# Attention scores in two fp32r passes with the query's two parts stacked in the rows, and the gate projection on four column tiles of the array

## The chip, the cores and the metric

The kernel runs on one NeuronCore of a Trainium2 chip. The metric is device time in microseconds (us) of one execution, lower is better; a kernel's time is the median over its runs. TensorE is called PE here (PEld is its weight load), VectorE DVE, ScalarE ACT, GpSimd POOL, and SP is the queue that issues most DMAs.

## The reference, cut to what matters

The program computes two transformer blocks of two layers each on 256 tokens of width 1024, in fp32. The change touches only the first layer of the first block. That layer projects the normed input `h` to 5,000-odd columns, sends one part through an mLSTM branch and the other through a sparse attention branch (NSA), and projects both back:

```python
proj = h @ w_in + b_in
ya = mlstm_branch(m_cols, ...)      # 4 + 4 gate columns: i_pre, f_pre
yb = nsa_branch(n_cols, ...)        # 24 gate columns: 8 heads x 3
...
s_s = jnp.einsum('bgrqd,bgqnd->bgrqn', q_blk, ks_g)   # selected keys
p_s = masked_softmax(s_s, tok_ok[:, :, None])
...
s_w = jnp.einsum('bgrqd,bgnd->bgrqn', q_blk, kwb)     # window keys
p_w = masked_softmax(s_w, wmask)
```

There are 8 query heads of 64 numbers in 2 groups; each group has its own keys. With 256 tokens both branches see all earlier tokens, so each is a plain causal attention over up to 256 keys. The 32 gate columns (4 input gates, 4 forget gates, 24 branch gates) are ordinary columns of `w_in`.

## The kernel before

**Layout.** Activations lie transposed: 128 partitions of features, 256 tokens in the free dimension, eight such slices for the width of 1024 (`xT`). A weight matrix is read in pieces of 128 x 1024; two pieces make one 1 MB DMA into a tile `raw` (three buffers, `load_raw`, L152). ACT rounds a piece to fp32r, `whi` (L161), DVE forms the rest, `wlo` (L162), and PE makes three one-pass products per 128 rows of the width: high by high, low by high, high by low (L221 to L223, or L206 to L208 where tokens are the output's rows). So one column tile of 128 columns costs one ACT cast, one DVE subtraction and 24 matmuls of 256 columns. Plain fp32 operands also can be multiplied; the trace shows such a matmul as two records.

**The layer.** `even_layer` (L391) runs over `EV_TILES` (L27), the order of its column tiles. `columns` (L458) projects them, `evict` (L411) scales the result by the token's norm (`norm.scaled`, tile `nt`, L310) and adds the bias. Tile `G` holds the 32 gate columns, spread to the rows 0 to 3, 32 to 35 and 64 to 87 of a 128-column tile whose other columns are zero; it goes to `gsb`. The mLSTM branch (`mlstm`, L521) and the attention (`nsa`, L597) are generators; `even_layer` runs their pieces between groups of column tiles.

**The attention.** `nsa` first normalises keys and queries in `nqk` (rows 0 to 63 are group 0, rows 64 to 127 group 1; slices 0 to 3 are the heads' queries, 4 the selected keys, 5 the window keys). `kblk` (L665) holds, for each group, its keys in its own 64 rows and zeros in the others, so that a matmul over all 128 rows with both groups' queries gives one group's scores. Then for two query blocks `qb` of 128 tokens, for four head pairs `j`, for two groups `g`: a score matmul (L748, 256 columns for the first block and 512 for the second), a mask (L749), the row maximum on DVE (L750, L751), two exponentials on ACT (L753), the scaling (L761, L763), transposes on PE (L769), a copy on ACT (`nPT`, L771) and the products with the values (tile `long`, L776, L777). Score and transpose share the two PSUM banks of `mbank(0)`.

**What sets the order.** Each engine works off its instructions in order. That order is not written by hand: the program is emitted in the order of the code with priorities, and a scheduler places each instruction by its own estimate of times. So a change in one place moves instructions on all engines behind it. `ada` (L338) is a long list of 96 DVE reductions over 512 KB weights (`araw`, L350, L351) that belong to the second block; `step` hands them out one by one from the first layer on, at raised priority, and `finish` forces them before they are needed.

**The layer behind.** `hgrn_layer` (L786) runs nine levels of small matmuls twice (L858, `hq`, `hk`, `hAC`), each between column tiles.

## Time and profile before

| | |
|---|---|
| median of 3 runs | 827.72 us (826.15 to 830.46) |
| profiled execution, its own time | 830.03 us |
| span in the profile | 828.2 us |
| mean granted clock of PE | 0.992 |
| PE busy | 807.2 us, 97% of the span |
| DVE busy | 672.1 us, 81% |
| ACT busy | 520.3 us, 63% |

"Busy" of PE is the time in which at least one matmul record is open, and records overlap, so it says when PE was fed and not that it ran at its peak. The granted clock is given as a share of 2.4 GHz. The chain of waits follows the execution back from its last instruction: each piece is what the piece after it waited for.

### The profile page before, as it was taken

The numbers are of one execution on the slowest core, as the hardware profiler recorded it, in microseconds if no ns is written. First come the engines' busy times: TensorE is split into PE (matmuls) and PEld (weight loads), VectorE is DVE, ScalarE is ACT, GpSimd is POOL, SyncE is SP. The second block draws the span as 40 slices with busy tenths as digits, with TensorE's granted clock in tenths as the row PEclk, the third lists the DMA queues.
The fourth block names the chain that finished last, engine by engine and source line by source line (L and its number), as shares of the span: only waits on it lengthen the run. The fifth ranks groups of instructions, "written<-read, shape, count | busy, mean of one in ns | idle before, by whom it ended". The sixth has DMA issues, their size and how long they took to land.

```text
span 828.2 us, 16357 instructions
## 1 busy us (share of the span) xinstructions
PE 807.2 (97%) x6534; PEld 740.2 (89%) x6534; DVE 672.1 (81%) x1257; ACT 520.3 (63%) x934; POOL 4.9 (1%) x19
## 2 busy tenths in 40 slices
PE   8999999989999999999999999999999999999995
PEld 8968977879999987999999888889999999988884
DVE  7689988899899989999999888876679777755552
ACT  7556765676876556658776734446657777754441
POOL 0000000001000000000000000000000000000000
PEclk9999999999999999999999999999999999999998
DMA  9644566657885777568878889874445454555521
GB/s 345 254 168 144 185 224 221 236 198 251 293 290 204 249 255 258 203 231 271 293 278 285 287 314 316 310 265 154 160 146 204 153 203 163 195 187 175 198 102 51
DMA packets 34635, 184.64 MB, mean 223 GB/s; under 512 B 3968, under 2 KB 4608, under 8 KB 19200
## 3 DMA queue, kind: packets, MB, share of 16 engines
q1 hardware_dynamic: 33696, 181.96, 62.8%
q10 hardware_dynamic: 864, 1.65, 0.6%
q8 instruction: 51, 0.84, 0.4%
q14 instruction: 24, 0.20, 0.1%
HBM read 182.55 MB, written 1.05 MB: 222 GB/s over the span
## 4 chain that ended last, share of the span: by engine, by line
PE 66%; DMA 13%; DVE 12%; ACT 5%; issue 4%; DVEq 0%; ACTq 0%; SPq 0%
PE g L221 12%; PE g L222 12%; DMA araw<-in_ada_w_dram 12%; PE g L223 12%; PE g L1035 9%; PE g L1036 5%; DVE wlo L162 4%; DVE araw L351 3%; ACT whi L161 2%; PE g L207 1%; PE g L208 1%; PE g L206 1%; PE m L858 1%; PE m L748 1%; PE long L776 1%
## 5 line engine op out<-in xcount | busy, mean ns | idle before, releaser
L221 PE MATMUL g<-ahi,whi 128*128 128x258 f32 (+1 forms) x1256 | 360.1, 289 | 4.0 <-ACT ahi L213 2.5
L222 PE MATMUL g<-alo,whi 128*128 128x258 f32 (+1 forms) x1256 | 357.6, 286 | 0.1
L223 PE MATMUL g<-ahi,wlo 128*128 128x258 f32 (+1 forms) x1256 | 356.6, 285 | 0.0
L162 DVE TENSOR_TENSOR wlo<-raw,whi 128x1024 fp32r<-128x1024 f32 (+1 forms) x238 | 288.6, 1216 | 73.5 <-ACT whi L161 72.9
L161 ACT CAST whi<-raw 128x1024 fp32r<-128x1024 f32 (+1 forms) x238 | 246.2, 1043 | 160.1 <-PE g L222 68.0
L221 PEld LDWEIGHTS g<-ahi,whi 128*128 128x128 f32 x1256 | 238.7, 191 | 8.7 <-ACT ahi L213 3.1
L222 PEld LDWEIGHTS g<-alo,whi 128*128 128x128 f32 x1256 | 240.2, 191 | 2.1 <-issue 0.8
L223 PEld LDWEIGHTS g<-ahi,wlo 128*128 128x128 f32 x1256 | 239.3, 191 | 1.7 <-issue 1.0
L1035 PE MATMUL g<-ghl,whi 128*128 128x512 f32 x512 | 179.9, 394 | 0.6 <-DVE nb L1020 0.6
L1036 PE MATMUL g<-ghl,wlo 128*128 128x256 f32 x512 | 143.5, 280 | 2.7 <-DVE wlo L162 2.4
L351 DVE CUSTOM_DVE_ANT_0 araw<-araw,row_c,prm 128x1024 f32<-128x1024 f32 x96 | 122.5, 1279 | 23.5 <-DMA araw<-in_ada_w_dram 23.3
L1035 PEld LDWEIGHTS g<-ghl,whi 128*128 128x128 f32 x512 | 96.0, 187 | 23.3 <-issue 0.7
L1036 PEld LDWEIGHTS g<-ghl,wlo 128*128 128x128 f32 x512 | 96.0, 187 | 4.0 <-DVE wlo L162 3.9
L310 DVE TENSOR_TENSOR nt<-g,nrstd 128x256 f32<-128x256 f32 x133 | 55.5, 419 | 17.3 <-PE g L223 16.9
L1021 ACT ACTIVATE nt<-nt,nb 128x256 f32<-128x256 f32 x64 | 32.4, 507 | 21.3 <-DVE nb L1020 21.3
L280 ACT ACTIVATE ahi<-xT,gains 128x256 fp32r<-128x256 f32 x32 | 16.2, 507 | 36.2 <-DVE xT L330 32.3
L214 DVE TENSOR_TENSOR ghl<-nt,ghl 128x256 fp32r<-128x256 f32 x64 | 27.0, 423 | 3.8 <-ACT ghl L213 1.4
L1022 ACT ACTIVATE nt<-nt 128x256 f32<-128x256 f32 x64 | 26.7, 418 | 1.9
L213 ACT CAST ghl<-nt 128x256 fp32r<-128x256 f32 x64 | 25.9, 406 | 1.9
L208 PE MATMUL g<-wlo,ahi 128*128 128x512 f32 (+1 forms) x64 | 24.3, 379 | 0.0
L206 PE MATMUL g<-whi,ahi 128*128 128x512 f32 (+1 forms) x64 | 24.2, 378 | 0.0
L286 ACT ACTIVATE sq<-xT 128x256 f32<-128x256 f32 x56 | 22.3, 405 | 3.0 <-DVE xT L330 3.0
(290 smaller groups left out, 758.7 us busy)
## 6 DMA issues: line engine op xcount, KB each, us to landing
raw<-in_mlp_w_dram SPq DMA_DIRECT2D x64, 1024.0 KB, 5.0
araw<-in_ada_w_dram SPq DMA_DIRECT2D x96, 512.0 KB, 5.1
raw<-in_ev_w_in_dram SPq DMA_DIRECT2D x17, 1024.0 KB, 6.1
raw<-in_od_w_in_dram SPq DMA_DIRECT2D x16, 1024.0 KB, 6.0
raw<-in_sgu_w_in_dram SPq DMA_DIRECT2D x8, 1024.0 KB, 4.7
raw<-in_ev_w_out_dram SPq DMA_DIRECT2D x4, 1024.0 KB, 4.9
raw<-in_od_w_out_dram SPq DMA_DIRECT2D x4, 1024.0 KB, 4.9
raw<-in_sgu_w_out_dram SPq DMA_DIRECT2D x4, 1024.0 KB, 4.7
```

The lines of the kernel that those rows point to most:

```text
L161: S.copy(hi[:, c], r[:, c])
L162: V.tensor_sub(lo[:, c], r[:, c], hi[:, c])
L206: PE.matmul(ps[tb], pair.hi(k)[:, ts_], wh[:, j, :], start=st, stop=False)
L208: PE.matmul(ps[tb], pair.hi(k)[:, ts_], wl[:, j, :], start=False, stop=sp)
L221: PE.matmul(ps, wh(k), ah(k), start=st, stop=False)
L222: PE.matmul(ps, wh(k), al(k), start=False, stop=False)
L223: PE.matmul(ps, wl(k), ah(k), start=False, stop=sp)
L310: V.tensor_tensor(t, ps[:, :T], self.r, op=ALU.mult)
L351: V.tensor_tensor_reduce(raw, raw, crow, 1.0, P("ada_b", layer * 48 + c), ALU.mult, ALU.add, mod[:, c : c + 1])
L1021: S.activation(r, r, AF.Relu, bias=b)
L1035: PE.matmul(ps, wh[:, k, :], a.rearrange("p s t -> p (s t)"), start=st, stop=sp, skip_group_check=True)
L1036: PE.matmul(ps[:, :T], wl[:, k, :], a[:, 0, :], start=False, stop=sp, skip_group_check=True)
```

## The change

Two things are changed, both in the first layer.

The scores: `q2` holds a query's rounded high part in the rows of its own group and the low part in the 64 rows of the other group, where `kblk` used to have zeros. `kblk` holds the keys' high part in both halves of the rows, and in a second slice their low part in both. Two fp32r matmuls, one per key part, give all four products. `q2` (in the memory of `cX`) is made for two head pairs at a time, by two ACT casts and two DVE subtractions of 64 x 256. `kblk` is made by six ACT copies and two DVE subtractions of 64 x 512 in place of a DVE memset and two DVE copies.

The gates: their 32 columns are loaded apart (`ev_w_g`, 128 KB, in the memory of `mE`), multiplied by the norm's gain on DVE, and projected with the unsplit `xT` by eight fp32 matmuls of 32 columns, four of them on the four column tiles of the array and four more added on top. A further fp32 matmul with a matrix of ones and zeros, `spread`, adds the four partial sums and puts each gate to its row. `G` leaves the column tiles, and with the padding tile that it needed, one 1 MB load and one split go.

```diff
-                if name == "G":
-                    V.tensor_scalar(gsb, t, gbias, None, op0=ALU.add)
...
+            def gates():
...
+                raw = mk(et, [128, 256], F32, "mE")
+                nc.sync.dma_start(raw, io["ev_w_g"])
+                wg = raw.rearrange("p (k n) -> p k n", n=32)
+                V.tensor_tensor(wg, wg, norm.gain[:, :, None].to_broadcast([128, KT, 32]), op=ALU.mult)
+                ps = gbank()[:, :T]
+                for k in range(KT):
+                    c = 32 * (k % 4)
+                    PE.matmul(ps[c : c + 32], wg[:, k, :], xT[:, k, :], start=k < 4, stop=k > 3, tile_position=(0, c))
+                t = norm.scaled(ps)
+                spread = mk(et, [128, 128], F32, "mqk")
+                G.memset(spread, 0.0)
+                for a, b, n in ((0, 0, 4), (32, 4, 4), (64, 8, 24)):
+                    S.copy(spread[:, a : a + n], lvl[:, 0, b : b + n])
+                pg = mbank(1)[:, :T]
+                PE.matmul(pg, spread, t, start=True, stop=True)
+                V.tensor_scalar(gsb, pg, gbias, None, op0=ALU.add)
...
-            columns(EV_TILES[6:11])
+            columns(EV_TILES[6:8])
+            gates()
+            columns(EV_TILES[8:10])
...
-        kblk = mk(ev, [128, 2, 2, T], F32, "kblk")
-        V.memset(kblk, 0.0)
+        kblk = mk(ev, [128, 2, 2, 2, T], F32R, "kblk")
         for g in range(2):
-            V.tensor_copy(kblk[64 * g : 64 * g + 64, g, :, :], nqk[64 * g : 64 * g + 64, 4:6, :])
+            own, other = slice(64 * g, 64 * g + 64), slice(64 - 64 * g, 128 - 64 * g)
+            k = nqk[own, 4:6, :]
+            for p in (own, other):
+                S.copy(kblk[p, g, 0], k)
+            V.tensor_sub(kblk[own, g, 1], k, kblk[own, g, 0])
+            S.copy(kblk[other, g, 1], kblk[own, g, 1])
...
+                if j % 2 == 0:
+                    q2 = mk(et, [128, 2, 2, 128], F32R, "cX", bufs=1)
+                    for g in range(2):
+                        own, other = slice(64 * g, 64 * g + 64), slice(64 - 64 * g, 128 - 64 * g)
+                        q = nqk[own, j : j + 2, qs]
+                        S.copy(q2[own, g], q)
+                        V.tensor_sub(q2[other, g], q, q2[own, g])
...
-                    PE.matmul(pv, nqk[:, j, qs], kblk[:, g, :, 0:n], start=True, stop=False)
+                    for part in range(2):
+                        PE.matmul(pv, q2[:, g, j % 2, :], kblk[:, g, part, :, 0:n], start=part == 0, stop=False)
```

How the order moves, at three places. On PE, where tile `G` ends and the tokens' tile `sv` begins (`g_464` is `G`'s bank, `g_498` that of `sv`; 21 more rows of `G` stand ahead of these), before:

```order
L221 MATMUL g_464<-ahi_129,whi_467 128x256
L222 MATMUL g_464<-alo_130,whi_467 128x256
L223 MATMUL g_464<-ahi_129,wlo_468 128x256
L206 MATMUL g_498<-whi_500,ahi_113 128x256
L207 MATMUL g_498<-whi_500,alo_114 128x256
L208 MATMUL g_498<-wlo_501,ahi_113 128x256
```

The same place now, from the last row of the tile ahead (`g_432`):

```order
L223 MATMUL g_432<-ahi_129,wlo_434 128x256
L481 MATMUL g_467<-xT_73,mE_464 32x256 x8
L206 MATMUL g_486<-whi_490,ahi_113 128x256
L207 MATMUL g_486<-whi_490,alo_114 128x256
L208 MATMUL g_486<-wlo_491,ahi_113 128x256
L206 MATMUL g_486<-whi_490,ahi_113 128x256
L207 MATMUL g_486<-whi_490,alo_114 128x256
L488 MATMUL m_85_483<-nt_476,mqk_478 128x256
L208 MATMUL g_486<-wlo_491,ahi_113 128x256
```

The 24 rows became eight and, five rows of `sv` later, the matmul with `spread`. On ACT, between the last copies of head pair 2 and the exponentials of head pair 3 of the first query block, before:

```order
L771 COPY nPT_1358<-m_242_1355 128x256
L771 COPY nPT_1368<-m_244_1365 128x256
L380 ACTIVATE mo_176<-nt_1742,hbias_181 128x256
L753 ACTIVATE A_1376,nsm_892<-m_248_1377,nnmx_891 128x128 x2
L580 ACTIVATE w_263_1445<-m_262_1443 128x256
```

Now:

```order
L806 COPY nPT_1367<-m_244_1364 128x256
L806 COPY nPT_1377<-m_246_1374 128x256
L777 CAST cX_1497<-nqk_177 64x256 x2
L788 ACTIVATE A_1385,nsm_885<-m_250_1386,nnmx_884 128x128 x2
L788 ACTIVATE A_1385,nsm_885<-m_251_1394,nnmx_884 128x128 x2
```

The two casts of `q2` for the second query block stand straight ahead of the exponentials. On DVE, at the maxima of head pair 2 of the second query block, before:

```order
L351 ISA araw_2316,mod_10_89<-araw_2316,row_c_396,prm_71 128x1024
L351 ISA mod_10_89 128x1
L750 TENSOR_REDUCE nmx_1459<-m_308_1624 128x2
L750 TENSOR_REDUCE nmx_1459<-m_309_1631 128x2
L751 TENSOR_SCALAR nnmx_1460<-nmx_1459 128x2
```

Now:

```order
L162 TENSOR_TENSOR wlo_1920<-raw_1881,whi_1919 128x1024
L785 TENSOR_REDUCE nmx_1470<-m_303_1594 128x2
L785 TENSOR_REDUCE nmx_1470<-m_304_1602 128x2
L786 TENSOR_SCALAR nnmx_1471<-nmx_1470 128x2
L778 TENSOR_TENSOR cX_1644<-nqk_177,cX_1644 64x256
L786 TENSOR_SCALAR nnmx_1471<-nmx_1470 128x2
L778 TENSOR_TENSOR cX_1644<-nqk_177,cX_1644 64x256
```

An `ada` reduction went from the place ahead of the maxima, and two subtractions of `q2` stand around the second bias. Over the whole DVE queue, 21 `ada` reductions stood ahead of the attention's first product with `nz` (L445) before and 17 stand there now; between that row and the last row of `hiv` (L846) in the next layer it is 27 and 28. On SP the load of the gate weights stands behind the third load of `ev_w_in`, and one load of `ev_w_in` fewer follows.

## Rows read from the trace of the kernel before

**Rows 1.** The page: busy of PE, and its granted clock in 40 slices.

```profile
PE 807.2 (97%) x6534; PEld 740.2 (89%) x6534; DVE 672.1 (81%) x1257; ACT 520.3 (63%) x934; POOL 4.9 (1%) x19
PEclk9999999999999999999999999999999999999998
```

**Rows 2.** Busy by stretch: length, then us busy and (records) of each engine, clock, DMA.

```profile
30.00:40.00 10.00, 10.00 (x86) 10.00 (x85) 5.51 (x9) 3.43 (x5) 0.00 (x0) 1.00 0.70 260
70.00:80.00 10.00, 10.00 (x65) 9.05 (x64) 9.56 (x28) 5.54 (x12) 0.20 (x2) 0.83 0.40 146
100.00:110.00 10.00, 10.00 (x73) 8.48 (x72) 9.65 (x24) 6.17 (x18) 0.00 (x0) 1.00 0.55 197
180.00:190.00 10.00, 8.32 (x61) 7.64 (x60) 9.19 (x21) 5.13 (x13) 0.00 (x0) 0.87 0.58 203
240.00:260.00 20.00, 19.82 (x464) 18.73 (x464) 19.97 (x37) 15.30 (x27) 0.00 (x0) 1.00 0.68 238
```

**Rows 3.** The chain of waits, 82 to 186 us: start, us, what (records).

```profile
107.08 0.43 PE m L748 x2
...
158.76 0.86 PE m L748 x2
...
161.56 1.56 ACT A L753 x7
...
183.36 0.60 ACT nout L780
```

**Rows 4.** Timeline of PE and DVE, 34 to 47 us: start, us, engine, line, operation.

```profile
34.55 0.28 PE L221 MATMUL g<-ahi,whi 128*128 128x256 f32 x1
...
37.40 0.28 PE L206 MATMUL g<-whi,ahi 128*128 128x256 f32 x1
...
42.98 0.28 PE L208 MATMUL g<-wlo,ahi 128*128 128x256 f32 x1
43.19 1.08 PE L643 MATMUL m<-raw,cX 128*32 128x128 f32 x32
44.20 1.12 PE L613 MATMUL m<-A,cst 128*128 128x512 f32 x2
...
45.85 0.39 PE L206 MATMUL g<-whi,ahi 128*128 128x512 f32 x1
46.08 0.39 PE L207 MATMUL g<-whi,alo 128*128 128x512 f32 x1
```

**Rows 5.** Groups by form, 0 to 260 us: busy us, mean ns, idle before.

```profile
L748 PE MATMUL m<-kblk,nqk 128*128 128x512 f32 x16 | 8.3, 613 | 0.0
L748 PE MATMUL m<-kblk,nqk 128*128 128x256 f32 x16 | 4.7, 386 | 0.0
L643 PE MATMUL m<-raw,cX 128*32 128x128 f32 x64 | 2.2, 275 | 1.2 <-issue 1.2
L643 PEld LDWEIGHTS m<-raw,cX 128*32 128x32 f32 x64 | 1.7, 109 | 1.7 <-issue 1.6
L161 ACT CAST whi<-raw 128x512 fp32r<-128x512 f32 x2 | 1.2, 618 | 1.7 <-DMA raw<-in_ev_w_dram 1.7
L162 DVE TENSOR_TENSOR wlo<-raw,whi 128x512 fp32r<-128x512 f32 x2 | 1.4, 692 | 1.7 <-ACT whi L161 1.7
L214 DVE TENSOR_TENSOR alo<-num,ahi 128x256 fp32r<-128x256 f32 x4 | 1.6, 420 | 0.1
L455 ACT ACTIVATE cpt<-nt,prm 64x256 f32<-64x256 f32 x4 | 2.0, 510 | 0.6 <-DVE nt L310 0.5
L351 DVE CUSTOM_DVE_ANT_0 araw<-araw,row_c,prm 128x1024 f32<-128x1024 f32 x35 | 44.7, 1277 | 4.3 <-DMA araw<-in_ada_w_dram 4.3
```

**Rows 6.** Waits, 60 to 200 us: engine, tile, line, waited for: us, times, longest.

```profile
ACT whi L161 <- PE g L222: 13.5, 10, 3.8
...
ACT A L753 <- DVE nnmx L751: 6.1, 4, 2.8
```

**Rows 7.** Timeline of DVE at 26 us, with the idle time ahead of it.

```profile
26.07 1.22 DVE L162 TENSOR_TENSOR wlo<-raw,whi 128x1024 fp32r<-128x1024 f32 x1 [2.14 <-ACT whi L161]
```

More of the change, by code (lines that the diff above doesn't have):

```diff
@@ L415, in evict @@
                 t = norm.scaled(ps)
-                if name == "G":
-                    V.tensor_scalar(gsb, t, gbias, None, op0=ALU.add)
-                elif kind in ("mq", "mk"):
+                if kind in ("mq", "mk"):
                     i += 4 * (kind == "mk")
@@ L500, in even_layer @@
             side.append(ada(crow))
-            columns(EV_TILES[11:17])
+            columns(EV_TILES[10:16])
             run(ns)
-            columns(EV_TILES[17:23])
+            columns(EV_TILES[16:22])
             early.append(1)
             run(ns)
-            columns(EV_TILES[23:25])
+            columns(EV_TILES[22:24])
             for n in (2, 1, 2, 0):
@@ L510, in even_layer @@
             early.clear()
-            columns(EV_TILES[25:31])
+            columns(EV_TILES[24:30])
             tab[0] = Table(EXP_LN, tab[0])
@@ L517, in even_layer @@
                 y.put(h, mout[:, h, :])
-            columns(EV_TILES[31:])
+            columns(EV_TILES[30:34])
             out_proj(io["ev_w_out"], y, add_x(nxt), 5, 2)
@@ L1262, in _pack @@
     for i, name in enumerate(EV_TILES):
+        if name == "G":
+            continue
         if name not in tok:
@@ L1267, in _pack @@
             ps.append(_pieces(_take(w, np.concatenate(tiles[i : i + n])), 8 // n, 128 * n))
-    a["ev_w_in"] = _paired(*ps, np.zeros((1, 128, 1024), f))
+    a["ev_w_in"] = _paired(*ps)
+    g0 = tiles[-1]
+    a["ev_w_g"] = np.ascontiguousarray(_pieces(_take(w, np.concatenate([g0[0:4], g0[32:36], g0[64:88]])), 8, 32)[0])
     first = a["ev_w_in"][0]
```

4 rows, old and new, of the table EV_TILES are left out of this document.

## The prediction, made before the result was known

> **What bounds the kernel now.** I read the page first: PE is open 807.2 of 828.2 us and its clock is at the full level in nearly every slice [rows 1]. So time comes off where PE gets less to do, unless something else is as late. Next I read the stretches of the first layer, where all of the change lies. There the reader should see two different stages. From 30 to 40 us PE is full, while DVE is at 5.51 and ACT at 3.43 of 10 us: only PE matters, and the gate tile lies there. From 70 to 190 us PE is still 8.3 to 10 of 10, but DVE is at 9.2 to 9.7 [rows 2]; the scores lie there, and I must ask which of the two ends last. The chain of waits answers for that stage. Score pairs are pieces of it, in the first query block (107.08) as in the second (158.76); at 161.56 it passes over to ACT and its exponentials, and it leaves the attention at the last copy, at 183.36 [rows 3]. So a shorter score is worth its length twice over: PE is in order and full, and the chain of the attention itself (score, maximum, exponential, transpose, value product) contains it. Twice PE ran at 1.2 instead of 2.4 GHz for a while, which shows as 0.83 and 0.87 in two stretches [rows 2].
>
> **The scores.** An fp32 matmul shows as two records. A pair takes 0.43 us at 256 columns and 0.86 us at 512 [rows 3]; there are eight instructions of each width (16 records each [rows 5]), so 8 x 0.43 + 8 x 0.86 = 10.3 us of PE. After the change there are 16 one-pass matmuls of each width. Their pitch is read from the weight tiles, which use the same type: tile `G` starts its 24 matmuls of 256 columns at 34.55 and hands over at 37.40, 0.119 us each, and two of 512 columns start 0.23 us apart (45.85 and 46.08) [rows 4]. That makes 16 x 0.119 + 16 x 0.23 = 5.6 us. **Gain 4.7 us.** If the scores are always covered by another wait, it is 0; more than 4.7 is not in these rows.
>
> **The price of `q2`.** Four preparations, each two ACT casts and two DVE subtractions of 64 x 256. No row has this cast; the nearest are 0.51 us (64 x 256 with a bias) and half of the 0.62 us of 128 x 512; I take 0.4. The subtraction is like that of 128 x 256, 0.42 us [rows 5]. That is 8 x 0.4 = 3.2 us on ACT and 8 x 0.42 = 3.4 us on DVE. Queued behind them are the exponentials on ACT and the second bias on DVE, for which PE's transposes wait. But the casts wait for the same score matmuls as the maxima, and the row maxima take longer than two casts; ACT stood waiting for the bias 6.1 us in four waits [rows 6], which is the cover. The subtraction between the biases is covered by the two exponentials of the first group. The first preparation has nothing of the scores ahead of it. On the path lie between 0 and 3 x 2 x 0.82 = 4.9 us; since the order puts the casts into ACT's wait, I take the low end plus one exposed subtraction: **cost 0.5 us.** If the cover is gone it costs the 4.9.
>
> **The price of `kblk`.** Six ACT copies of 64 x 512, by the 0.62 us of 128 x 512 at most 3.7 us, and two DVE subtractions at 0.69 us, in place of two DVE copies and a memset that ran at the start. The copies go ahead of two weight casts, so PE could starve for `whi`. Against it: ACT waits for PE to free a weight buffer, 13.5 us in ten waits [rows 6], so the casts run ahead of PE. That row begins at 60 us and the copies stand just before, so the bounds are 0 and 3.7. I take 0.
>
> **The gates.** Removed: the 24 matmuls, 37.40 - 34.55 = 2.85 us of a full PE. Added: eight fp32 matmuls, 16 records of 256 columns. The kernel has column tiles of 32 already, in L643: 32 records of 128 columns run from 43.19 to 44.20 [rows 4], so 0.032 us each where a lone fp32 record of 128 columns would be half of a 0.43/2 record, 0.11. Four run abreast. As many columns in all make 1.01 us here too, plus 0.09 for the change of tiling (42.98 to 43.19 against the pitch of 0.119). The matmul with `spread` is one fp32 pair of 256 columns, 0.43 us, and it waits for DVE's scaling; five matmuls of `sv`, 0.6 us, are put ahead of it, and matmul end plus scaling is 0.28 + 0.42, so 0.1 to 0.3 us stay exposed; 0.2. Sum 1.73. **Gain 1.1 us**; were the column tiles serial, 16 x 0.215 = 3.4 us instead of 1.1, it would be a loss of 1.2 us.
>
> The loads of L643 take 109 ns each, and 64 of them cover 1.7 us while their matmuls cover 2.2 us [rows 5]: loads run under matmuls although all use all 128 rows. The Trainium skill (TensorE: Matmul & The Clock Gate, "Packing small matmuls — row/col tiling") says that a weight load overlaps running matmuls only when its row group differs; by that rule each of the four rounds would first load for 0.11 us, the gates would take 0.44 us more and the forecast below would be 822.8 us; the trace of L643 disagrees, since the loads' 1.7 us and 64 records x 0.11 / 4 = 1.8 us of columns would be 3.5 us one after the other, and its matmuls are open 2.2 us.
>
> Beside PE: the gate tile's split goes (one ACT cast, one DVE subtraction), off the path by the 5.51 and 3.43 of 10 us. The gain product on DVE (128 x 256, 0.42 us) waits for the gate weights' DMA and holds up one scaling and one weight split behind it. Their cover is DVE's own idle time, 2.14 us before the split at 26.07, which waits for the weight load ahead of it in the same queue [rows 7]. Cost 0, and 0.4 us if that is gone. SP loads 1 MB less ahead of the attention, which may bring the next weights sooner; bounds 0 and the 1 or 2 us around 42 to 47 us, where PE waits for other things as well; I take 0.
>
> **What moves.** Four `ada` reductions leave the DVE queue ahead of the attention's end (21 to 17), 1.28 us each [rows 5]: DVE gets 5.1 us less there, and 3.4 us of `q2` more. So DVE does not become the bound in that stage. In the next layer it has one more than before (27 to 28) where it is busy 19.97 of 20 us [rows 2]; between 0 and 1.3 us. PE is at 19.82 there. I take 0.
>
> **The sum.** 4.7 + 1.1 - 0.5 = 5.3 us off the profiled execution: 830.03 becomes 824.7, its span 828.2 becomes 822.9. That execution was 2.3 us over the median, so against 827.72 the forecast is **822.4 us**.
>
> **Rivals.**
> *The scores are covered.* If ACT and DVE set the pace of each head pair, the shorter score only lengthens PE's wait. For it: DVE at 9.65 of 10 and the chain's passage through ACT after 160 us. Against it: the chain takes PE's score pairs up to 158.76 [rows 3]. Then only the gates count: 827.72 - 1.1 = 826.6, or 827.1 with the 0.5 of `q2`.
> *DVE in the next layer (slower).* Place: the nine levels from 240 us on, where DVE has no idle time left. If the four displaced reductions come due there, 4 x 1.28 = 5.1 us is late, and PE's level matmuls wait for DVE's masks. With the scores covered as well the time is 827.72 - 1.1 + 5.1 = 831.7, and 0.5 for `q2` makes 832.2. It decides from one reduction (1.3 us, more than the gates' gain) on. Against it: the order shows only one more.
> *The column tiles don't run abreast* (the change does not do what it says): 822.4 + 2.3 = 824.7.
> *More falls away.* A new PE order that loses the spell at the low clock at 70 to 80 us gains (1 - 0.83) x 10 = 1.7 us [rows 2], and a shorter wait for weights at 42 to 47 us as much; together 819.
>
> **How the numbers follow.** The forecast gets 0.55, the covered scores 0.20, DVE in the next layer 0.10, serial column tiles 0.05, more falling away 0.10. About 0.5%, 4.1 us, can be told from no change here, so faster means below 823.6. The forecast lies 1.2 us under that, and its unknowns (4.9 for `q2`, 3.7 for `kblk`, a new order on all engines) are mostly costs, so a quarter to a third of it falls into "same": 0.40 faster, 0.15 same. Faster: 0.40 + 0.10 + a little of the others = 0.52. Slower: 0.10. The rest, 0.38, is the same. The range for 8 in 10 goes from 817.0, the last rival with another order's 2 us, to 828.0, the covered scores with 1 us of new waits.
>
> **What would show it.** Score records: twice 16 of 0.12 and 0.23 us pitch instead of pairs of 0.43 and 0.86. The gate stage from nq3's last matmul to `sv`'s first: 1.1 us instead of 2.85. The last copy of the attention at about 178 us instead of 183.36. If that copy comes earlier but the end does not, the next layer took it back; look at DVE from 240 us on. If it does not come earlier, look at ACT's waits ahead of the exponentials and at the casts of `q2`. The forecast is wrong if ACT or DVE shows less waiting per head pair than before while PE waits more.

## The result, and the profile after

The change made the kernel slower. Its median is 837.27 us (11 runs, 833.20 to 842.55); the kernel before, on the same chip, has 827.72 us (11 runs). The ratio of the two is **1.0109, 95% interval 1.0085 to 1.0132**, or 9.0 us. Forecast were 822.4 us and a range up to 828.0.

The profiled execution of after took 842.55 us (span 840.8), the longest of its 11, so its rows show the losses rather too large. First the page: busy of each engine, and PE's granted clock in 40 slices.

```profile
PE 806.4 (96%) x6528; PEld 742.6 (88%) x6528; DVE 674.5 (80%) x1264; ACT 525.4 (62%) x950; POOL 5.1 (1%) x20
PEclk8999999999999999999999999989999999999998
```

PE is open 0.8 us less than in [rows 1], in a span that is 12.6 us longer: it now waits where it did not. The stretches say where, in the columns of [rows 2]. First after the change:

```profile
70.00:80.00 10.00, 8.25 (x61) 7.17 (x60) 9.14 (x25) 4.94 (x10) 0.00 (x0) 0.99 0.17 56
110.00:120.00 10.00, 8.70 (x50) 6.83 (x48) 7.22 (x18) 4.74 (x18) 0.00 (x0) 0.83 0.59 195
180.00:190.00 10.00, 7.64 (x53) 7.19 (x53) 7.71 (x20) 4.49 (x11) 0.00 (x0) 0.83 0.69 253
190.00:200.00 10.00, 7.17 (x43) 6.55 (x42) 7.26 (x18) 5.56 (x10) 2.69 (x2) 0.83 0.64 236
240.00:260.00 20.00, 17.12 (x360) 16.35 (x359) 18.89 (x32) 14.10 (x24) 0.00 (x0) 0.91 0.68 231
560.00:570.00 10.00, 7.74 (x29) 6.61 (x30) 4.26 (x6) 2.80 (x4) 0.00 (x0) 0.66 0.61 210
```

Three of these stretches before it:

```profile
110.00:120.00 10.00, 10.00 (x70) 8.22 (x70) 8.37 (x21) 6.08 (x21) 0.00 (x0) 1.00 0.55 179
190.00:200.00 10.00, 9.81 (x79) 9.61 (x79) 9.01 (x19) 8.10 (x16) 2.71 (x2) 0.96 0.74 265
560.00:570.00 10.00, 9.90 (x79) 9.38 (x78) 6.53 (x13) 7.49 (x12) 0.00 (x0) 1.00 0.38 118
```

At 70 us PE had 10.00, at 180 us 8.32 and at 240 us 19.82 [rows 2]. Each of these stretches has lost PE time, and in most of them the clock is below 1 as well (before, it was 0.83 at 70 us and 0.87 at 180 us): a mean of 0.83 over 10 us is 1.7 us lost beside the waiting. Over whole runs the granted clock is 0.983 on average after the change (11 runs) and 0.992 before it (the 22 runs that e1 to e4 are held against). One minus the clock, times the span, is 14.1 us against 6.5 us; so up to 7.6 of the 9.0 us show as a lower clock. It is a bound, since PE does not work in all of that time. Between executions of one and the same kernel, a us of this reckoning went with about 0.5 us of time (177 runs of after and e1 to e18) to 0.8 us (121 runs of before), with much scatter; by that, an estimate, the clock carries 4 to 6 of the 9.0 us.

The removed work did go. These are the groups by form, 0 to 260 us, as in [rows 5]: the scores, the gates, and the preparation of `q2`.

```profile
L783 PE MATMUL m<-kblk,cX 128*128 128x512 f32 x16 | 5.5, 448 | 0.0
L783 PE MATMUL m<-kblk,cX 128*128 128x256 f32 x16 | 3.5, 320 | 0.0
L481 PE MATMUL g<-xT,mE 128*32 128x256 f32 x16 | 1.1, 385 | 0.0
L777 ACT CAST cX<-nqk 64x256 fp32r<-64x256 f32 x8 | 3.2, 400 | 2.9 <-PE m L783 2.8
L778 DVE TENSOR_TENSOR cX<-nqk,cX 64x256 fp32r<-64x256 f32 x8 | 3.4, 420 | 0.3
```

Score records are open 9.0 us instead of 13.0 [rows 5], and casts and subtractions have the durations that the prediction took. The gates' place on PE, the timeline:

```profile
35.15 0.28 PE L223 MATMUL g<-ahi,wlo 128*128 128x256 f32 x1
35.36 1.07 PE L481 MATMUL g<-xT,mE 128*32 128x256 f32 x16
36.37 0.39 PE L206 MATMUL g<-whi,ahi 128*128 128x256 f32 x1
...
36.94 0.28 PE L207 MATMUL g<-whi,alo 128*128 128x256 f32 x1
37.14 0.67 PE L488 MATMUL m<-nt,mqk 128*128 128x256 f32 x2
37.46 0.47 PE L208 MATMUL g<-wlo,ahi 128*128 128x256 f32 x1
```

From the end of `nq3` (35.15 + 0.12) to the first matmul of `sv` it is 1.10 us, where the tile took 2.85 [rows 4]; the matmul with `spread` adds 0.40 (37.06 to 37.46). The four column tiles run abreast. The Trainium skill (TensorE: Matmul & The Clock Gate, "Packing small matmuls — row/col tiling") lets a weight load overlap only where the row group differs; here 16 loads of 0.11 us each, 1.76 us end to end, all on the same 128 rows, lie in 1.01 us together with their matmuls, which does not agree with it.

So why is it slower? The longest waits of PE from 60 to 260 us (us in total, times, longest), the chain of waits at the first long one, and what stands at the end of the first mlp:

```profile
PE g L221 <- ACT ahi L213: 2.9, 2, 2.4
PE m L893 <- DVE hq L935: 2.9, 1, 2.9
PE g L223 <- DVE wlo L162: 1.9, 2, 1.7
PE g L221 <- DVE wlo L162: 1.9, 1, 1.9
PE m L609 <- ACT w L607: 1.3, 1, 1.3
```

```profile
75.09 1.05 ACT whi L161
...
76.94 0.50 ACT qk L423
77.47 0.48 DVE qk L425
77.95 1.15 DVE wlo L162
79.14 0.39 PE g L223
```

```profile
555.80 1.28 DVE L351 CUSTOM_DVE_ANT_0 araw<-araw,row_c,prm 128x1024 f32<-128x1024 f32 x1 [0.72 <-DMA araw<-in_ada_w_dram]
...
557.13 1.28 DVE L351 CUSTOM_DVE_ANT_0 araw<-araw,row_c,prm 128x1024 f32<-128x1024 f32 x1
...
562.26 1.22 PE L294 MATMUL m<-sq,ones 128*128 128x256 f32 x2 [4.18 <-DVE sq L289]
```

Two subtractions of `q2` (75.13 and 75.89) stand on DVE ahead of that first wait, but they are not pieces of its chain: DVE stands idle for 0.70 us behind them until ACT has `qk` (L423) ready, and the weight split stands behind the row that needs it (L425). On the whole chain of this execution there is no subtraction of `q2`.

The last two of the 96 `ada` reductions stand on DVE at 556 to 558 us, ahead of the squares of the norm at the mlp's end, and PE waits 4.18 us. Before, the last one began at 540.3 us and PE had no wait there.

### The profile page after: what moved, and what is told of

Read it like the earlier page. It is cut to its first block, busy times and chain, and to the rows that moved or that the text cites. A ratio compares the mean times of both kernels' runs of the same rounds, so it can differ in the third digit from the quotient of the medians.

```text
span 840.8 us, 16380 instructions
## 1 busy us (share of the span) xinstructions
PE 806.4 (96%) x6528; PEld 742.6 (88%) x6528; DVE 674.5 (80%) x1264; ACT 525.4 (62%) x950; POOL 5.1 (1%) x20
## 4 chain that ended last, share of the span: by engine, by line
PE 76%; DVE 8%; DMA 6%; issue 2%; ACT 1%; DVEq 0%; SPq 0%; ACTq 0%
PE g L221 16%; PE g L223 15%; PE g L222 15%; PE g L1070 12%; PE g L1071 6%; DMA araw<-in_ada_w_dram 6%; DVE wlo L162 2%; DVE araw L351 2%; PE m L893 1%; PE long L811 1%; PE m L294 1%; DMA raw<-in_od_w_in_dram 1%; PE m L783 1%; PE m L804 1%; PE g L206 0%
## 5 line engine op out<-in xcount | busy, mean ns | idle before, releaser
L162 DVE TENSOR_TENSOR wlo<-raw,whi 128x1024 fp32r<-128x1024 f32 (+1 forms) x237 | 286.8, 1215 | 74.2 <-ACT whi L161 73.8
L207 PE MATMUL g<-whi,alo 128*128 128x512 f32 (+1 forms) x64 | 24.2, 379 | 0.0
```

The costliest lines, as they stand in the source:

```text
L162: V.tensor_sub(lo[:, c], r[:, c], hi[:, c])
```

## The experiments

A word on the order: the text ahead of the prediction says that `step` hands out the reductions at raised priority. The experiments show that its offset of -50 puts them back: at 50 more stand ahead of the attention's end (21 in e10, 19 in e2, which differ by the offset alone). Three counts from the order on DVE describe a kernel below: the reductions ahead of the attention's first product with `nz`, those ahead of the next layer's levels, and the weight splits (L162) ahead of the last reduction. Before they are 21, 32, 144 of 237; after, 17, 29, 147 of 236.

All ratios are to runs of the kernel before on the same chip. The runs of one kernel spread over 4 to 12 us, so sizes are taken from the ratios (0.001 is 0.83 us), and the single profiled execution is used for places. e4, e6 and e7 have four runs each, e13 and e18 six, e3 seven.

| kernel | ratio | 95% interval | mean clock |
|---|---|---|---|
| after | 1.0109 | 1.0085 to 1.0132 | 0.983 |
| e1 scores' part alone | 1.0038 | 1.0006 to 1.0069 | 0.991 |
| e2 gates' part alone | 1.0021 | 1.0000 to 1.0042 | 0.993 |
| e3 before, reductions later | 1.0077 | 1.0045 to 1.0109 | 0.989 |
| e4 after, reductions earlier | 1.0190 | 1.0146 to 1.0234 | 0.984 |
| e5 after, reductions as before | 1.0071 | 1.0035 to 1.0107 | 0.990 |
| e6 before + both preparations | 1.0107 | 1.0033 to 1.0182 | 0.986 |
| e7 after, subtractions on POOL | 1.0145 | 1.0069 to 1.0221 | 0.984 |
| e8 after, scores twice | 1.0059 | 1.0022 to 1.0095 | 0.988 |
| e9 before, another offset | 0.9984 | 0.9969 to 1.0000 | 0.994 |
| e10 gates, reductions as before | 1.0014 | 0.9994 to 1.0034 | 0.992 |
| e11 before, scaling on ACT | 0.9972 | 0.9948 to 0.9996 | 0.992 |
| e12 after, scaling on ACT | 1.0041 | 1.0015 to 1.0067 | 0.989 |
| e13 before + `q2` | 1.0096 | 1.0061 to 1.0132 | 0.985 |
| e14 before + `kblk` | 1.0027 | 1.0006 to 1.0049 | 0.993 |
| e15 scores, `q2` made once | 1.0046 | 1.0028 to 1.0065 | 0.986 |
| e16 e9 and e11 together | 0.9983 | 0.9961 to 1.0006 | 0.993 |
| e17 before + casts of `q2` | 1.0001 | 0.9984 to 1.0018 | 0.993 |
| e18 scores, reductions as in e6 | 1.0066 | 1.0047 to 1.0084 | 0.987 |

**The reductions.** e3 hands them out later in the kernel before; e4 earlier in the changed one.

```diff
             columns(EV_TILES[17:23])
-            early.append(1)
             run(ns)
```

> The kernel before, with the ada reductions handed out later: no step is taken between the pieces of the attention. Nothing else is changed. On DVE 18 reductions stand ahead of the attention's first product with nz (21 before, 17 after) and the last stands behind 150 weight splits (144 before, 147 after). Theory A (the backlog): the last reductions come due ahead of the norm at the end of the first mlp, PE stalls there by 4 us or more and runs at half clock for some us behind it as after the change: 833 to 838 us. Theory B (the attention itself) and a theory that the lighter PE loses its clock: nothing of the change is in this kernel, so 826 to 829 us.

```diff
                     if early:
-                        step(2)
+                        step(3)
+                        step(3)
...
-            early.clear()
             columns(EV_TILES[24:30])
             tab[0] = Table(EXP_LN, tab[0])
             run(ml)
             run(ns)
+            early.clear()
```

> The changed kernel, with the ada reductions handed out earlier: two steps instead of one between the pieces of the attention, and up to its end. On DVE 24 reductions stand ahead of the attention's first product with nz (21 before, 17 after), and the last stands behind 137 weight splits (147 after). Theory A (the backlog): the stall ahead of the norm at the end of the first mlp (4.2 us, and 3.2 us at half clock behind it) goes, and the waits around 182 to 250 us shrink: 825 to 830 us. Theory B (the attention itself): the loss lies ahead of 182 us and DVE gets more to do there, 837 to 842 us.

Measured: 1.0077 and 1.0190. PE's longest wait of e3 from 470 to 582 us, then that of e4 in the same stretch, then the longest two of e4 from 60 to 345 us:

```profile
PE m L294 <- DVE sq L289: 4.6, 1, 4.6
```

```profile
PE g L221 <- DVE nb L1056: 0.2, 1, 0.2
```

```profile
PE g L221 <- DVE nt L310: 5.8, 1, 5.8
PE g L223 <- DVE wlo L162: 3.7, 5, 1.7
```

e3 makes the stall of after in a kernel that has nothing of the change, and costs 6.4 us (3.7 to 9.0): theory A holds for that place. e4 takes the stall away and is still worse, by 15.7 us against before, at the upper end of what theory B said: PE waits for DVE in the attention instead, whose last copy comes at 189.55 (183.36 before [rows 3]). So theory A alone falls. No place that was tried for the reductions is free; that DVE is as late as PE in both stages (theory D) would explain it. The stall follows the third count: in the profiles PE waits there 0 us with 137 splits ahead (e4), 0.4 with 143 (e5), 0.7 and 2.2 with 145 (e2, e8), 1.0 with 146 (e1), 4.2 and 4.5 with 147 (after, e7), 4.6 with 150 (e3).

**Each part alone.** e1 takes the attention of after with the gates of before, e2 the reverse; both are cut from the diff of the change.

> The scores' part alone: attention as after the change, gates and column tiles as before it. Theory A (the backlog): the loss comes from the ada reductions that were handed out later; each is late on DVE, and the last ones hold up the norm at the end of the first mlp. On DVE 18 reductions stand ahead of the attention's first product with nz here (21 before, 17 after), and the last of the 96 stands behind 146 weight splits (144 before, 147 of one split fewer after). So A expects about half of the change's loss: 829 to 833 us, and a stall of PE ahead of that norm shorter than the 4.2 us it had after the change. Theory B (the attention itself): the casts and subtractions of q2 and kblk hold up ACT and DVE by more than the score matmuls give back. B expects nearly the whole loss, 835 to 838 us, with the attention's last copy no earlier than the 182.0 us of after.

> The gates' part alone: gates as after the change, scores, kblk and q2 as before it. On DVE 19 reductions stand ahead of the attention's first product with nz (21 before, 17 after), the last of the 96 behind 145 weight splits of 236. Theory A (the backlog): a gain of about 1 us in the gate stage and a loss of 1 to 4 us from the two displaced reductions: 827 to 831 us. Theory B (the attention itself): the gates are innocent, 826.5 us, the 1.1 us gain that was forecast. Theory C (any new order costs some us, whatever stands in it): 831 to 835 us.

Measured: 1.0038 and 1.0021, +3.1 and +1.7 us. Neither gains, and together they make 4.9 of the 9.0 us. The rest appears only with both parts; that it comes from the order, which the parts share, is likely and not shown. The gates were not the 1.1 us gain.

**Reductions put back, price of the preparations, DVE relieved, scores made longer.** e5:

```diff
-            with tc.high_priority(offset=-50):
+            with tc.high_priority(offset=50):
```

and `early.clear()` moved as in e4.

> The changed kernel with the ada reductions brought back to their places of before: steps are taken up to the attention's end and at raised priority. On DVE 20 reductions stand ahead of the attention's first product with nz (21 before, 17 after), 32 ahead of the first level of the next layer (32 before, 29 after), and the last of the 96 stands behind 143 of 236 splits (144 of 237 before, 147 of 236 after). Theory A (only the late reductions cost): the stall of 4.2 us ahead of the norm at the mlp's end goes with its 3.2 us at half clock, and the forecast's gain is there: 821 to 829 us. Theory D (DVE is as late as PE from 63 us on, so that a reduction costs wherever it stands): the mlp's stall goes, but the attention and the next layer are later by 3 to 6 us than after the change: 832 to 838 us.

e6, in the kernel before (`q2` as in the change, not read; `kboth` takes the place of the new `kblk`):

```diff
+        kboth = mk(ev, [128, 2, 2, T], F32R, "kboth")
+        for g in range(2):
...
+                S.copy(kboth[p, g], k)
+            V.tensor_sub(kboth[own, g], k, kboth[own, g])
+            S.copy(kboth[other, g], kboth[own, g])
...
+                        S.copy(q2[own, g], q)
+                        V.tensor_sub(q2[other, g], q, q2[own, g])
```

> The kernel before, with the casts and subtractions of q2 and kblk made as after the change, but not used: the scores stay fp32 (kblk's preparation goes into a tile of its own of half the size). The reductions stand as before from the next layer on (32, and 144 splits), 19 instead of 21 ahead of the attention's end. So this is the price of the preparations alone. The forecast's price was 0.5 us. Theory A: 827.5 to 829 us. Theory B (the preparations hold up ACT and DVE) and theory D (DVE gets 4.8 us more and is as late as PE): 831 to 834 us.

e7, in after:

```diff
-            V.tensor_sub(kblk[own, g, 1], k, kblk[own, g, 0])
+            G.tensor_sub(kblk[own, g, 1], k, kblk[own, g, 0])
...
-                        V.tensor_sub(q2[other, g], q, q2[own, g])
+                        G.tensor_sub(q2[other, g], q, q2[own, g])
```

> The changed kernel, with the ten subtractions of q2 and kblk moved from DVE to POOL, which is idle in that stage: 8 x 0.42 and 2 x 0.69 us less on DVE. The reductions stand exactly as after the change (17, 29, 147 splits). Theory D (DVE is as late as PE): 3 to 5 us earlier at the attention's end, 832 to 834 us. Theory A (only the late reductions cost): the stall at the mlp's end is still there, 836 to 838 us. If POOL's subtractions are much longer than DVE's, the scores wait for them, and the time is above that of after.

e8, in after:

```diff
-                    for part in range(2):
-                        PE.matmul(pv, q2[:, g, j % 2, :], kblk[:, g, part, :, 0:n], start=part == 0, stop=False)
+                    for i in range(4):
+                        PE.matmul(pv, q2[:, g, j % 2, :], kblk[:, g, i % 2, :, 0:n], start=i % 2 == 0, stop=i == 1)
```

> The changed kernel with each score's two matmuls made twice (the second pair starts the sum anew), which gives PE 5.6 us more in the attention, about what the change had taken off it. The order also moves: 19 reductions ahead of the attention's end, the last behind 145 splits. If PE is what the attention waits for, 837 + 5.6 = 843 us. Theory D (DVE is as late as PE): the added matmuls lie in PE's waits; no more than 1 to 2 us, 836 to 839 us. Theory C (the lighter PE loses its clock, whoever waits): fewer spells at half clock than the seven of after, and 828 to 834 us.

Measured: 1.0071, 1.0107, 1.0145, 1.0059.
- e5 is 3.1 us under after (about -0.4 to 6.7): so much is the estimate for the displaced reductions, and not all of the loss.
- e6 is the surprise: the preparations alone, with no gain to set against them, cost 8.9 us (2.7 to 15.1), more than any theory said.
- e7 did not relieve anything: its stall at the mlp's end is there (4.5 us), and one subtraction takes 0.74 us on POOL where DVE takes 0.42. Why its median is above after's, by an interval that reaches it, is open.
- e8 has 5.2 us more of open score records than after (14.2 instead of 9.0) and is faster than it, by 4.1 us (about 0.5 to 7.7). By the ratio, 832.5 us, it lies in the range of theory C (a lighter PE loses its clock), under that of theory D, and its profile has five spells at half clock ahead of the end against seven. But its last reduction also stands two splits earlier, and its stall is 2.2 us instead of 4.2. e13 below loses nearly as much clock (0.985) with the old scores, so a lighter PE is not needed for the loss; whether it adds to it in after is open.

**Controls and a relief of DVE on ACT.** e9 is before with `offset=0`; e10 is e2 with `offset=50`; e11 is before, and e12 is after, with

```diff
-                        if g:
-                            V.tensor_scalar(x, x, r, None, op0=ALU.mult)
-                        else:
-                            S.mul(x, x, r)
+                        S.mul(x, x, r)
```

> A control: the kernel before with one number changed, the priority at which the ada reductions are handed out (offset 0 instead of -50). Every operation is the same, and the counts too: 21 reductions ahead of the attention's first product with nz, 32 ahead of the next layer's levels, the last of the 96 behind 144 splits; single rows on DVE change places in the attention. Theory D (the time follows DVE's work ahead of the attention's end and the place of the last reductions): nothing of it is changed, within 1.5 us of before, 826 to 830 us. Theory C (any new order costs some us): 831 to 836 us.

> The gates' part alone, with the ada reductions put back to their places of before by a higher priority (offset 50): 21 and 32 ahead of the two marks, the last behind 143 of 236 splits (144 of 237 before). Theory A and D: the loss of the gates' part alone was the displacement, so its gain of about 1 us shows now: 825.5 to 828 us. Theory C (any new order costs): 830 to 834 us.

> The kernel before, with the scaling of the second group's exponentials moved from DVE to ACT, 16 instructions, 4.3 to 5 us less on DVE and 7.5 us more on ACT in the attention. The last reduction stands behind 144 splits as before, 22 instead of 21 ahead of the attention's end. Theory D (the attention's length follows DVE's work): DVE has about 3 us less there net of the reduction, and the attention ends 2 to 3 us earlier, 824 to 827 us. If ACT is as late as DVE there, 828 to 832 us.

> The changed kernel with the same scaling moved from DVE to ACT. By it the scheduler itself puts the reductions back: 19 ahead of the attention's first product with nz (17 after), 32 ahead of the next layer (29 after), the last behind 143 splits (147 after, 144 of 237 before). Theory D: DVE has 4.5 us less and the stall at the mlp's end is gone, so 6 to 10 us less than after, 827 to 831 us. Theory C (any new order costs) or ACT as the bound of the attention: 833 to 838 us.

Measured: 0.9984, 1.0014, 0.9972, 1.0041. e9 shows another order that costs nothing, so "any new order is slower" falls. e11 gains 2.3 us (0.3 to 4.3) by taking 4.3 us off DVE, although ACT gets 5.5 us more of them; theory D expects that. e12 brings the changed kernel from 1.0109 to 1.0041, but it also puts the reductions back (19, 32, 143), as e5 does; against e5 it is 2.5 us faster, within the noise, so the relief itself is not shown there. e10 has no gain from the gates with the reductions at their old places; its interval excludes the forecast 1.1 us by little.

**Which preparation, and are the scores covered?** e13 has `q2` of e6 alone, e14 `kboth` alone. e17 is e13 without the line of the subtraction. e15 is e1 with `q2` made once:

```diff
+        q2 = mk(et, [128, 2, 2, 128], F32R, "cX", bufs=1)
...
+            q = nqk[own, 0:2, 0:128]
+            S.copy(q2[own, g], q)
+            V.tensor_sub(q2[other, g], q, q2[own, g])
         yield
         for qb in range(2):
...
-                if j % 2 == 0:
-                    q2 = mk(et, [128, 2, 2, 128], F32R, "cX", bufs=1)
```

e16 joins e9 and e11. e18 is e1 with `offset=0` and `early.clear()` moved as in e4, which gives it e6's counts (19, 32, 144).

> The kernel before with q2's four preparations made but not used (the scores stay fp32), and nothing of kblk. On DVE 19 reductions stand ahead of the attention's first product with nz (21 before), 32 ahead of the next layer's levels and the last behind 144 splits, both as before. With kblk's preparation as well the time was 837 us, 8 to 9 us above before. If q2 is the dear part (its instructions stand in ACT's and DVE's queues between scores and exponentials): 831 to 835 us. If kblk is the dear part: 827 to 829 us.

> The kernel before with kblk's preparation made but not used (six ACT copies and two DVE subtractions of 64 x 512), and nothing of q2. The reductions stand exactly as before (21, 32, 144 splits). The forecast bounded this price at 0 to 3.7 us and took 0. In all kernels with it the stage from the values' projection to the first maxima was about 1.3 us longer. If that is all: 828 to 830 us. If kblk is the dear part of the preparations: 832 to 835 us.

> The scores' part alone, with the gates as before, where q2 is made once, ahead of the first score, and used for all head pairs: three of its four preparations are left out, so the scores are those of wrong queries. The reductions stand nearly as before (20, 32, 144 splits). So it shows the shorter scores with kblk's preparation and one of q2's. Scores on the path, as forecast: 4.7 us less for the scores and at most 2 us for the rest, 824 to 826 us. Theory D (DVE is as late as PE, scores covered): no gain, 828 to 830 us.

> The kernel before with the two edits that did not make it slower: the ada reductions handed out at offset 0 instead of -50, and the scaling of the second group's exponentials moved from DVE to ACT. 22 reductions ahead of the attention's first product with nz, 32 ahead of the next layer, the last behind 144 splits. Theory D: DVE gets 4.3 to 5 us less in the attention and nothing is displaced: 823 to 826 us. If the two gains of 1 us were order alone: 826 to 829 us.

> The kernel before with only the ACT half of q2's preparation: eight casts of 64 x 256, 0.4 us each, unused; the eight DVE subtractions are left out. The reductions stand exactly as before (21, 32, 144 splits). With the subtractions q2 alone cost 8 us. If the subtractions are the dear half (they stand ahead of a weight split on DVE at 75 us, and PE waits 1.8 us for that split and then runs at half clock): 827 to 829 us here. If the casts are (ahead of ACT's weight casts and exponentials): 833 to 836 us.

> The scores' part alone with the ada reductions as in the kernel that has the preparations but keeps the fp32 scores: 19 ahead of the attention's first product with nz, 32 ahead of the next layer, the last behind 144 splits in both. So the two differ by the score matmuls alone, 4.7 us of PE. That kernel was 8 to 9 us above before. If the forecast's gain is on the path once the order is held: 4 to 5 us less than that, 831 to 833 us. If the scores are covered: 835 to 837 us.

Measured: `q2` 1.0096, `kblk` 1.0027, casts alone 1.0001. (e14 keeps the old copies of `kblk`, 0.8 us of DVE that the change removes, so its 2.2 us may be too much.) So in the kernel before the dear half is the **eight DVE subtractions of `q2`: 7.9 us, for 3.4 us of DVE time**, with what the scheduler moves on their account (19 reductions instead of 21 ahead of the attention's product). The two traces differ where the first two stand. DVE in e13, then in e17:

```profile
74.55 0.26 DVE L724 TENSOR_REDUCE nmxc<-m 128x8 f32<-128x120 f32 x1
74.84 0.42 DVE L750 TENSOR_TENSOR cX<-nqk,cX 64x256 fp32r<-64x256 f32 x1
75.29 0.28 DVE L728 TENSOR_TENSOR nEc<-m,nmxc 128x120 f32<-128x120 f32 x1
75.60 0.42 DVE L750 TENSOR_TENSOR cX<-nqk,cX 64x256 fp32r<-64x256 f32 x1
76.06 0.48 DVE L427 SCALAR_TENSOR_TENSOR qk<-mqk,prm,qk 128x256 f32<-128x256 f32 x1
76.46 1.22 DVE L162 TENSOR_TENSOR wlo<-raw,whi 128x1024 fp32r<-128x1024 f32 x1
```

```profile
72.72 0.26 DVE L724 TENSOR_REDUCE nmxc<-m 128x8 f32<-128x120 f32 x1
72.91 1.20 DVE L162 TENSOR_TENSOR wlo<-raw,whi 128x1024 fp32r<-128x1024 f32 x1
74.04 2.45 DVE L427 SCALAR_TENSOR_TENSOR qk<-mqk,prm,qk 128x256 f32<-128x256 f32 x6
```

Behind the same reduction (L724) the weight split follows after 0.2 us in e17 and after 1.9 us in e13. Of that, 0.84 us are the two subtractions; the rest is L728 and a row of L427, which the new order also puts ahead of the split. (e13 is 1.8 us later here already; 1.6 of it stand at 10 us, ahead of anything that differs.) The chain of waits of e13 passes through both subtractions and the split to PE. PE waits 1.79 us for this split in e13 and has no wait for it in e17 (74.17); e17 waits 0.84 us for the next split, and its clock stays. PE in e13, then in e17:

```profile
77.73 0.58 PE L223 MATMUL g<-ahi,wlo 128*128 128x256 f32 x1 [1.79 <-DVE wlo L162]
78.11 0.41 PE L221 MATMUL g<-ahi,whi 128*128 128x256 f32 x1
78.32 0.41 PE L222 MATMUL g<-alo,whi 128*128 128x256 f32 x1
```

```profile
73.91 0.23 PE L560 MATMUL m<-mnegbf,identbf 128*128 128x128 bf16 x1
74.17 0.39 PE L223 MATMUL g<-ahi,wlo 128*128 128x256 f32 x1
...
77.87 0.39 PE L223 MATMUL g<-ahi,wlo 128*128 128x256 f32 x1 [0.84 <-DVE wlo L162]
78.09 0.28 PE L221 MATMUL g<-ahi,whi 128*128 128x256 f32 x1
78.21 0.28 PE L222 MATMUL g<-alo,whi 128*128 128x256 f32 x1
```

The next starts lie 0.21 us apart in e13 and 0.12 in e17: 1.2 and 2.4 GHz. A wait of 1.75 us for the same split stands in the profiles of after, e4, e5, e8 and e12, each time with a lower clock at it or behind it. There the subtractions stand ahead of the split as well, but in all five DVE then waits 0.7 us for ACT, as shown above for after: it is the place of the split behind that row that PE pays for. So what e13 measures is the price of `q2` in the kernel before; that the changed kernel pays it in the same way is not shown. In e13 PE waits again at 113 us (0.9 us, for ACT) and at 194 us (1.8 us, for ACT), with the lower clock behind it. Its mean clock is 0.985 against 0.993 in e17, or 7 us by the reckoning above, a bound; with the 0.5 to 0.8 us of time per us, about half of the 7.9 us passes through the clock, an estimate.

e18 is 3.4 us under e6 with the same counts. Between them lie the score matmuls, the old copies of `kblk` (in e6 alone) and e18's other hand-out of the reductions. That speaks for scores on the path once the preparations are there. It is no proof: e6's interval is 6 us to either side, e15 showed no gain (its one preparation, all at one place, brought a PE wait of 2.9 us and a low clock with it), and e8 speaks against. The scores' worth stays open between 0 and 5 us. e15 shows one thing more: with six of the eight subtractions left out it lies above both of its forecasts and is no faster than e1 (1.0046 and 1.0038), so the 7.9 us is no price per subtraction; it depends on where they come to stand.

e16 is not faster than e9 or e11 alone; the two edits do not add up. The fastest kernel here is e11, 0.28% under before with an interval that ends just under 1.

## Why the prediction was wrong

A ladder of four steps orders the case (ratio times 827.6 us): before to e6, the preparations, **+8.9**; e6 to e18, the short scores, **-3.4**; e18 to e5, the gates, **+0.4**; e5 to after, the displaced reductions, **+3.1**. That the sum is the +9.0 says nothing, since each step starts where the last one ended. Only the first is clear of the noise, and it is borne out by e13 and e14 (7.9 + 2.2); each of the other three has an interval that reaches 0. The steps from e6 on also move the offset or `early.clear()`.

- *What bounds the kernel.* PE "full" was read rightly, and the work taken off it was there: 9.0 us of score records instead of 13.0. But PE at 10 of 10 with DVE at 9.2 to 9.7 [rows 2] was read as PE's stage with DVE as an onlooker, since DVE would have less to do by sum. By sum it did: from 60 to 180 us it is busy 107.80 us after the change and 108.65 before. But it had half a us in ten to spare, and what counts there is which rows stand ahead of a split that PE needs.
- *The price of `q2`* is **the step that failed**: 0.5 us forecast, bounds 0 to 4.9; put alone into the kernel before, it measured 7.9 (e13, 5.0 to 10.9). The durations were right (0.40 and 0.42 us), and the casts' cover held (e17: nothing). The subtractions were looked at only inside the attention, between the biases. "The first preparation has nothing of the scores ahead of it" was true, and beside the point: on DVE it stands ahead of a weight split, and the column tile on PE waits for that. And no bound held the clock: a wait of 1.8 us was priced as 1.8 us, not with the 1.7 us that PE loses behind it (3.4 us at half clock in e13). How the changed kernel comes to its loss is shown less well: no subtraction of `q2` lies on its chain, and neither e7 nor e15, which take all or most of them off DVE, gave time back. What its trace shows is a new order in which splits and reductions stand where PE waits for them; which part of the change brings each of these places stays open.
- *The price of `kblk`*: 0 forecast, bounds 0 to 3.7, measured 2.2 (0.5 to 4.1). The value taken was the low end of the bounds, and they hold the measured one. On the chain of after one of its subtractions is a piece of 0.55 us (at 56.60).
- *The gates*: the stage was forecast at 1.1 + 0.63 us and took 1.10 + 0.40. Yet e2, e10 and e18 to e5 show +1.7 (0 to 3.5), +1.2 (-0.5 to 2.8) and +0.4 us, none a gain. Where the 1.3 us are given back was not found.
- *What moves*: taken at 0; 3.1 us by e5 (about -0.4 to 6.7), and 6.4 us in e3, which only hands the reductions out later. The rival "DVE in the next layer" had the mechanism (late reductions, covered scores, above 831 us) and a chance of 0.10. Its price, 5.1 us, came out by luck: from the second projection of the mlp to the first product with `vt` it was 143.7 us before and 148.7 after, but that is a stall of 4.2 us and the half clock behind it, less waits that went, and not four reductions' length. Its place was right in part: PE does wait for DVE at 242 us (2.9 us for `hq`, behind two reductions), but a larger piece came due 300 us later, at the norm that closes the mlp. The count was followed up to the end of the next layer and not to the point where the last reduction is due.
- *What would show it* worked: the last copy of the attention came at 181.99 instead of 178, still 1.4 us earlier than before. The sentence on that case points to the next layer, and the profile of after does lose its time behind that copy: it is 4.2 us late at the first `hq` (230.9, before 226.7), 7.4 us at the mlp's second projection (471.5, before 464.1) and 12.5 us at the first product with `vt` (620.3, before 607.8).
- *The 1 MB less on SP* was not tried by itself.

## What to carry to other kernels

Where two engines are both above 90% in a stage, an edit that moves work from one to the other has to be costed on the one that receives it: list what stands behind each new instruction in its queue, for the whole kernel and not only for the chain that it belongs to. A busy time that stays the same says nothing on this. Work that a scheduler spreads over idle places has a date by which it is due; count at that date, since what is displaced in one stage may be paid two stages later. And on PE a wait of one to two us can cost as much again behind it. Last, a price measured in the old kernel need not be the one that the new kernel pays: look for the new instructions on the chain of waits of both.

## What the runs showed of the hardware

- Waits of PE of 0.9 to 1.85 us were sometimes followed by matmuls at a pitch of 0.21 instead of 0.12 us: of 74 such waits between 60 and 600 us in the 20 profiles, 21 had the lower clock begin in them or within 2 us behind, and of 40 waits of 1.7 us and more, 26. A wait of 2.5 us that began at 98.6 us in e5 and one of 1.75 us at 325 us in e1 had none behind them, and the spell of before at 75 us [rows 2] has no wait ahead of it in the trace. What decides was not settled.
- Casts to fp32r of 64 x 256 on ACT, eight of 0.4 us, cost nothing that e17 can tell (0.1 us, within 1.4 either way) in a stage where ACT is busy 5 to 6 us of 10 [rows 2]; eight subtractions of the same size and 0.42 us on DVE cost 7.9 us, about twice their length, in the order that they brought.
- A subtraction of 64 x 256 takes 0.74 us on POOL (median of e7's eight; one took 1.6) and 0.42 on DVE; one of 64 x 512 took 1.27 and 1.56 us on POOL and 0.65 on DVE.
